# A four-layer diffusion trunk step: two projections as one f32 product each, one mask less, norm weights as columns, a shorter inverse root

## The chip, the cores and the metric

One core of one Trainium2 chip runs one program that holds the whole step. The metric is device time in microseconds (us) from the first to the last instruction of the core, with what lies around it; lower is better. Times of the kernel before are the median of three runs and one profiled execution.

## The reference

128 prompt tokens (s = 0) and 128 sample tokens (s = 1) of width 1024 go through four layers. Layer 0 mixes tokens with a gated DeltaNet, layer 1 with neighbourhood attention, layer 2 with latent attention (low-rank keys and values), layer 3 with RWKV-7. Each layer then applies a SwiGLU feed-forward of inner width 2816. Before each sub-layer stands a root-mean-square norm, modulated by a shift and scale from an adaptive matrix (`ada_w`). All inputs are float32. The parts that the change touches:

```python
def rmsnorm(x, g):
    y = x * lax.rsqrt(jnp.mean(x * x, -1, keepdims=True) + NORM_EPS)
    return y * g
...
# every sub-layer: x += gate * f(rmsnorm(x) * (1 + scale) + shift)
def chunk_gated_delta(q, k, v, g, beta, s0):
    ...
    a_mat = jnp.where(strict, jnp.einsum('...id,...jd->...ij', kb, k) * decay, 0.0)
    sol = lax.linalg.triangular_solve(a_mat + jnp.eye(DN_CHUNK), rhs, left_side=True, lower=True, unit_diagonal=True)
...
def deltanet_mixer(h, s0, w_in, w_gate, ..., out_norm, w_out):
    q, k, v, z = jnp.split(h @ w_in, 4, -1)
    ...
    o = rmsnorm(o, out_norm) * jax.nn.silu(z.reshape(b, t, DN_HEADS, DN_DIM))
    return o.reshape(b, t, -1) @ w_out, s
...
def na_project(h, w_qkv, q_norm, k_norm):
    qkv = (h @ w_qkv).reshape(b, t, 3, NA_HEADS, NA_DIM).transpose(2, 0, 3, 1, 4)
    return rmsnorm(qkv[0], q_norm), rmsnorm(qkv[1], k_norm), qkv[2]
...
def mla_project(h, w_a, q_a_norm, kv_a_norm, w_q_b, q_norm):
    cq, ckv, kpe = jnp.split(h @ w_a, [MLA_Q_LORA, MLA_Q_LORA + MLA_KV_LORA], -1)
    q = (rmsnorm(cq, q_a_norm) @ w_q_b).reshape(b, t, MLA_HEADS, MLA_NOPE + MLA_ROPE)
    return rmsnorm(q, q_norm).transpose(0, 2, 1, 3), rmsnorm(ckv, kv_a_norm), kpe
...
def rwkv_step(s, inp):
    r, w, k, v, a, bb = inp
    sa = jnp.einsum('...ij,...j->...i', s, a)
    s = s * w[..., None, :] + sa[..., :, None] * bb[..., None, :] + v[..., :, None] * k[..., None, :]
    return s, jnp.einsum('...ij,...j->...i', s, r)
...
    return (y * g) @ w_out, s        # end of rwkv_mixer
```

## The kernel before, in words

**One recorded program.** The Python code does not issue instructions directly. A `Recorder` (L84) writes every engine operation to a `Tape` (L64); `Plan` (L1753) then sorts all operations of all engines with a table of engine costs and free buffers, over several rounds (`Plan.best`, L2071), and `emit` issues the order that it judges best, all from L2133. So every instruction of the profile has one line, and a change of one operation sorts the whole program anew: work with no dependence on its neighbours, above all the adaptive matrix, can move by hundreds of instructions.

**Products.** A large projection is kept near float32 accuracy in three fp32r products. `weight` (L304) loads a 128x1024 piece over SyncE's queue, and `split` (L285) makes two halves of it: ScalarE copies the raw weight to fp32r (hi), VectorE subtracts that from the raw weight (lo). `linear` (L320) then issues, for each of two token groups and each k tile of 128, hi·hi, hi·lo and lo·hi, each a matmul with 512 columns. The activations are split in the same way (`norm_T` L456, `to_T` L414, `split_T` L422). `linear_k` (L377) has a mode `whole` already: one f32 product on the raw weight, used for RWKV's r, k and v. `out_half` (L481) is the projection out of a mixer, half of its input width at a time, whose result `residual` (L486) adds to x.

**Filler.** `ada_group` (L243) computes the adaptive matrix: for each k tile four concurrent matmuls of 32 stationary and 512 moving columns, with 1 MB of `ada_w` per load. Nothing in the mixer waits for it, so the planner puts it where TensorE would be idle.

**Norms and inverse roots.** `normed` (L432) reads the sums of squares, calls `rsqrt` (L149) for a 128x1 column, scales x and transposes it. `rsqrt` is 11 VectorE instructions: a scaled sum, a shift and a multiply-add on the bits, and two rounds of four.

**DeltaNet** (`deltanet_`, L704). `linear` at L866 computes z (chunks 6 and 7 of `dn_w_in`) and its gate. `inverses` (L650) inverts the triangular matrices of the delta rule: ScalarE gathers 32x32 diagonal blocks, VectorE transposes them (`inverse_base`, L586) and does a substitution of 31 steps with two instructions each (`substitute`, L602), then TensorE continues with 32x32 and 64x128 products. TensorE can do other work only if the planner has some left.

**Attention** (`neighbourhood_` L1044, `latent_` L1139). `rms_heads` (L976) multiplies each head by its inverse root and then by the norm's weight, both on VectorE; `transposed` (L984) transposes heads on TensorE and copies them out of PSUM on ScalarE.

**RWKV-7** (`rwkv_`, L1255). It works in two halves of the heads (g = 0, 1). `rw_products` (L1614) forms key products AT, which VectorE multiplies by a strict triangular mask out of PSUM; `inverses` is used on these too, once per half; `rw_core` (L1629) solves and applies the state, `rw_out` (L1713) normalises, and `out_half` projects with `rw_w_out` (L1494, L1502).

## Time and profile before

| what | value |
|---|---|
| timed runs | median 1655.51 us (1654.04 to 1658.28, three runs) |
| profiled execution | 1659.55 us, span of the core 1657.8 us |
| TensorE (PE) busy | 1577.0 us, 95% of the span, 11320 records |
| weight loads (PEld) busy | 1295.8 us, 78% |
| VectorE (DVE) busy | 1097.0 us, 66% |
| ScalarE (ACT) busy | 811.7 us, 49% |
| mean granted TensorE clock | 0.978 |

The trace gives, for each instruction, start, length, and what released it if its engine had been idle; "v" stands for any tile of the program, since tile names carry numbers. A matmul of f32 operands leaves two records in PE and two weight loads in PEld, one of fp32r operands one each. The records of both say "f32".

### The profile page before, as it was taken

Reading aid. Unit: us, or ns where it says so; the run is one execution under the profiler, and the core shown is the slowest. Engines: PE = TensorE matmul, PEld = TensorE weight load, DVE = VectorE, ACT = ScalarE, POOL = GpSimd, SP = SyncE. Lnnn points to the kernel's source line nnn. Section 1 sums busy time; section 2 is a strip of 40 time slices with the busy share of each in tenths; the row PEclk is TensorE's granted clock in tenths of the full one; section 3 lists DMA queues with packets and bytes.
Section 4 is the critical chain, followed back from the end, with each engine's and each line's share of the span. In section 5 each row is a group of like instructions: output and inputs, shape, how many; then the busy total and the mean of one; then the engine's idle time right before and its main releaser. Section 6 shows DMA issues by size and latency. Waiting matters only on the chain. (4 is left out here: it accounts for less than half of the span.)

```text
span 1657.8 us, 28812 instructions
## 1 busy us (share of the span) xinstructions
PE 1577.0 (95%) x11320; PEld 1295.8 (78%) x11320; DVE 1097.0 (66%) x2294; ACT 811.7 (49%) x1405; POOL 71.7 (4%) x137
## 2 busy tenths in 40 slices
PE   7999699999999999999999999999999699989998
PEld 3986377998778779987776799885757388879986
DVE  4887786444597874455997744547883898765444
ACT  4795365434466763344666644433633442454343
POOL 2001010000002000000110000000000000000000
PEclk9999799999999999999999999999999879999999
DMA  9768787558667675566767845666071421345554
GB/s 353 276 242 290 290 274 280 190 153 288 225 246 189 232 260 152 167 203 201 262 196 265 292 153 166 215 207 238 16 292 41 158 87 62 100 151 154 166 191 140
DMA packets 132792, 334.03 MB, mean 201 GB/s; under 512 B 18465, under 2 KB 32594, under 8 KB 121392
## 3 DMA queue, kind: packets, MB, share of 16 engines
q1 hardware_dynamic: 125936, 311.33, 54.9%
q0 software_dynamic: 6720, 20.86, 4.4%
q8 instruction: 89, 1.46, 0.4%
q14 instruction: 47, 0.39, 0.1%
HBM read 328.25 MB, written 3.90 MB: 200 GB/s over the span
## 5 line engine op out<-in xcount | busy, mean ns | idle before, releaser
L2133 PE MATMUL v<-v,v 128*128 128x256 f32 (+12 forms) x11288 | 1571.5, 331 | 74.9 <-DVE v L2133 34.2
L2133 PEld LDWEIGHTS v<-v,v 128*128 128x128 f32 (+8 forms) x11288 | 1290.1, 173 | 354.0 <-issue 123.9
L2133 DVE TENSOR_TENSOR v<-v,v 128x512 f32<-128x512 f32 (+16 forms) x1244 | 856.1, 714 | 480.9 <-ACT v L2133 328.3
L2133 ACT ACTIVATE v<-v 128x1024 fp32r<-128x1024 f32 (+14 forms) x972 | 674.6, 732 | 782.1 <-PE v L2133 316.1
L2133 ACT ACTIVATE v<-v,v 128x128 f32<-128x128 f32 (+2 forms) x172 | 65.6, 434 | 21.7 <-DVE v L2133 14.0
L2133 ACT ACTIVATE v<-v,v,v 128x128 f32<-128x128 f32 (+2 forms) x136 | 55.8, 495 | 35.1 <-DVE v L2133 34.2
L2133 DVE SCALAR_TENSOR_TENSOR v<-v,v,v 128x128 f32<-128x128 f32 (+4 forms) x152 | 59.1, 446 | 6.0 <-ACT v L2133 3.8
L2133 DVE TENSOR_REDUCE v<-v 128x4 f32<-128x512 f32 (+4 forms) x76 | 47.0, 626 | 8.3 <-PE v L2133 4.8
L2133 POOL DMA_DIRECT2D v<-v x22 | 11.8, 539 | 765.8 <-DVE v L2133 405.0
L2133 DVE TENSOR_SCALAR v<-v 128x1 int32<-128x1 int32 (+11 forms) x202 | 35.0, 177 | 6.2 <-ACT v L2133 3.7
L2133 DVE SCALAR_TENSOR_TENSOR v<-v,v 128x4 f32<-128x4 f32 (+6 forms) x172 | 34.0, 211 | 5.2 <-ACT v L2133 3.3
L2133 POOL MEMSET v<- 128x512 f32 (+6 forms) x49 | 21.4, 446 | 365.5 <-DVE v L2133 143.1
L2133 DVE SCALAR_TENSOR_TENSOR v<-v 128x1 f32<-128x1 f32 (+4 forms) x171 | 26.4, 162 | 1.9
L2133 DVE STREAM_TRANSPOSE v<-v 128x1024 f32<-128x1024 f32 x12 | 23.5, 2009 | 5.4 <-ACT v L2133 5.2
L2133 DVE TENSOR_SCALAR v<-v,v,v 128x128 f32<-128x128 f32 x64 | 24.7, 405 | 3.3 <-PE v L2133 2.9
L2133 ACT ACT_TABLE_LOAD x18 | 23.1, 1283 | 4.0 <-DVE v L2133 3.0
L2133 DVE TENSOR_SCALAR v<-v,v 128x512 f32<-128x512 f32 (+2 forms) x68 | 24.3, 389 | 0.2
L2133 DVE TENSOR_TENSOR v<-v 128x1 f32<-128x1 f32 (+4 forms) x74 | 11.8, 160 | 11.2 <-ACT v L2133 10.2
L2133 DVE COPY v<-v 128x32 f32<-128x32 f32 (+7 forms) x23 | 4.9, 211 | 13.3 <-PE v L2133 13.1
L2133 ACT ACTIVATION_READ_ACCUMULATOR v<-v,v 128x1 f32 x64 | 13.3, 207 | 0.0
L2133 DVE RECIPROCAL v<-v 128x2 f32<-128x2 f32 (+2 forms) x25 | 4.5, 181 | 7.7 <-ACT v L2133 7.6
L2133 POOL DMA_DIRECT2D v<-rw_w x10 | 6.0, 601 | 59.4 <-DVE v L2133 58.5
(38 smaller groups left out, 62.6 us busy)
## 6 DMA issues: line engine op xcount, KB each, us to landing
v<-ada_w SPq DMA_DIRECT2D x88, 1024.0 KB
v<-ffn_w_in SPq DMA_DIRECT2D x160, 512.0 KB
v<-ffn_w_out SPq DMA_DIRECT2D x88, 512.0 KB
v<-dn_w_in SPq DMA_DIRECT2D x32, 512.0 KB
v<-na_w_qkv SPq DMA_DIRECT2D x24, 512.0 KB
v<-rw_w_rkv SPq DMA_DIRECT2D x24, 512.0 KB
v<-v POOLq DMA_DIRECT2D x20, 512.0 KB, 4.9
v<-ada_w SPq DMA_DIRECT2D x16, 512.0 KB
```

Source lines behind the costliest of these rows:

```text
L2133: ins = getattr(getattr(nc, engine), method)(*[real(a) for a in args], **{k: real(a) for k, a in kw.items()}).ins
```

## The change

It has four parts. First, `WHOLE = ("dn_z", "rw_out")`: z of DeltaNet and RWKV's projection out become one f32 product on raw weights; `norm_T` keeps the unsplit activations for it, and RWKV's output is no longer split. (The diff also offers the same for the projections of latent attention, which is not switched on.) Second, `rw_products` copies AT out of PSUM on ScalarE without the mask. Third, the weights of the q and k norms become columns that scale ScalarE's copy in `transposed`; the multiplies of VectorE stay only where the new cache needs the weighted keys (two in neighbourhood attention) and for the 32 rotated columns of the sample tokens in latent attention (four of 128x4x32). Seven small loads on GpSimd's queue fill the columns. Fourth, `rsqrt` merges the shift into the multiply (minus a half), and for a single column needs three instructions a round: 8 instead of 11, and 10 instead of 11 elsewhere.

```diff
         with self.scope():
             m, y, t, v = [self.g(shp) for _ in range(4)]
-            h, yi = t.bitcast(I32), y.bitcast(I32)
-            nc.vector.tensor_scalar(m, x, scale / k ** 2, eps / k ** 2, op0=OP.mult, op1=OP.add)
-            nc.vector.tensor_scalar(h, m.bitcast(I32), 1, None, op0=OP.logical_shift_right)
-            nc.vector.tensor_scalar(yi, h, -1.0, float(0x5f3759df), op0=OP.mult, op1=OP.add)
+            single = shp[1] == 1
+            carry = k ** 6 if single else k ** 2
+            nc.vector.tensor_scalar(m, x, scale / carry, eps / carry, op0=OP.mult, op1=OP.add)
+            nc.vector.tensor_scalar(y.bitcast(I32), m.bitcast(I32), -0.5, float(0x5f3759df), op0=OP.mult, op1=OP.add)
             for last in (False, True):
+                if single:
+                    f = k if last else 1.0
+                    nc.vector.scalar_tensor_tensor(t, y, y, m, op0=OP.mult, op1=OP.mult)
+                    nc.vector.scalar_tensor_tensor(v, t, -10.0 / 3 / f, t, op0=OP.add, op1=OP.mult)
+                    nc.vector.scalar_tensor_tensor(out if last else y, v, 5.0 / f ** 2, y, op0=OP.add, op1=OP.mult)
+                    continue
                 if last:
...
-    def linear(self, W, chunks, xs, evac, lags=None):
+    def linear(self, W, chunks, xs, evac, lags=None, whole=False):
...
-                held[t] = self.weight([W[k0 * 128:(k0 + n) * 128, a:b] for a, b in chunks[ci]], n, width)
-            hi, lo = held[t]
+                held[t] = (self.raw_weight if whole else self.weight)([W[k0 * 128:(k0 + n) * 128, a:b] for a, b in chunks[ci]], n, width)
             if k0 == 0:
                 acc[s] = self.ps()[:, :width]
             for kk in range(n):
                 k = k0 + kk
+                if whole:
+                    nc.tensor.matmul(acc[s], xs[s](k), held[t][:, kk, :], start=(k == 0), stop=(k == nk - 1))
+                    continue
+                hi, lo = held[t]
                 xh, xl = xs[s](k)
...
+        if lo is None:
+            self.nc.scalar.activation(hi, v, AF.Copy, **({} if gain is None else {"scale": gain}))
+            return
...
+                if keep:
+                    h = hs[g][:, :, s]
+                else:
+                    own = self.g([128, 4, 128])
+                    h = own
...
-    def out_half(self, W, oT, g, gates):
-
-        xs = [lambda k, s=s: (oT[0][g][:, k, s, :], oT[1][g][:, k, s, :]) for s in range(2)]
-        self.linear(W[g * 512:g * 512 + 512], [[(0, 512)], [(512, 1024)]], xs, self.residual(gates, g == 1), OUT)
+    def out_half(self, W, oT, g, gates, whole=False):
+
+        xs = [lambda k, s=s: oT[0][g][:, k, s, :] if whole else (oT[0][g][:, k, s, :], oT[1][g][:, k, s, :]) for s in range(2)]
+        self.linear(W[g * 512:g * 512 + 512], [[(0, 512)], [(512, 1024)]], xs, self.residual(gates, g == 1), OUT, whole)
...
+WHOLE = ("dn_z", "rw_out")
...
-        self.linear(W, [[(c * 512, c * 512 + 512)] for c in (6, 7)], xs, gating, IN)
-        self.free(ht)
+        if "dn_z" in WHOLE:
+            self.free(ht)
+            self.linear(W, [[(c * 512, c * 512 + 512)] for c in (6, 7)], [lambda k, s=s: hs[k // 4][:, k % 4, s] for s in range(2)], gating, IN, True)
+            self.free(hs)
+        else:
+            self.linear(W, [[(c * 512, c * 512 + 512)] for c in (6, 7)], xs, gating, IN)
+            self.free(ht)
...
-        nc.vector.tensor_tensor(x, x, gain[:, None, :].to_broadcast([128, nh, hd]), op=OP.mult)
+        if gain is not None:
+            nc.vector.tensor_tensor(x, x, gain[:, None, :].to_broadcast([128, nh, hd]), op=OP.mult)
...
-        nc.scalar.activation(dst, p[:w, :n * 128].rearrange("p (a b) -> p a b", b=128), AF.Copy)
+        nc.scalar.activation(dst, p[:w, :n * 128].rearrange("p (a b) -> p a b", b=128), AF.Copy, **({} if gain is None else {"scale": gain}))
...
-        gq, gk = self.g([128, 64]), self.g([128, 64])
-        self.bcast_row(gq, I["na_q_norm"][j])
+
+        for i, nm in enumerate("qk"):
+            for e in range(2):
+                nc.gpsimd.dma_start(gc[64 * e:64 * e + 64, i:i + 1], I[f"na_{nm}_norm"][j].rearrange("(p o) -> p o", o=1))
+        nc.vector.tensor_scalar(gc[:, 0:1], gc[:, 0:1], 0.125, None, op0=OP.mult)
...
-                self.rms_heads(heads(t), 8, 64, gq if ci < 2 else gk)
+                own = ci >= 2 and s == 0
+                self.rms_heads(heads(t), 8, 64, gk if own else None)
                 g = slice(ci % 2 * 4, ci % 2 * 4 + 4)
                 dst = qT[s][:, g] if ci < 2 else k0T[:, g] if s == 0 else k1T[ci % 2][:, :, 0]
-                self.transposed([t[:, i * 128:(i + 1) * 128] for i in range(4)], 4, dst)
...
+        nc.gpsimd.memset(gc, 1.0)
+        nc.gpsimd.dma_start(gc[0:96, 0:1], I["mla_q_norm"][j].rearrange("(p o) -> p o", o=1))
+        nc.gpsimd.dma_start(gc[0:64, 2:3], I["mla_k_norm"][j, 0:64].rearrange("(p o) -> p o", o=1))
+        nc.vector.tensor_scalar(gc[0:96, 0:1], gc[0:96, 0:1], gc[0:96, 2:3], 96 ** -0.5, op0=OP.mult, op1=OP.mult)
+        nc.vector.tensor_copy(gc[0:64, 1:2], gc[0:64, 0:1])
...
-                self.rms_heads(q, 4, 96, gq)
+                self.rms_heads(q, 4, 96)
                 if s == 1:
+                    nc.vector.tensor_tensor(q[:, :, 64:96], q[:, :, 64:96], gq[:, None, :].to_broadcast([128, 4, 32]), op=OP.mult)
                     self.rope(q[:, :, 64:96], 4)
-                self.transposed([q[:, i] for i in range(4)], 4, qT[s][ci // 2][:96, ci % 2 * 4:ci % 2 * 4 + 4])
+                self.transposed([q[:, i] for i in range(4)], 4, qT[s][ci // 2][:96, ci % 2 * 4:ci % 2 * 4 + 4], gc[:96, s:s + 1])
...
-                nc.vector.tensor_tensor(f["AT"][s][e], p[e].rearrange("p (i t) -> p i t", i=4),
-                                        self.K(f"mstr{d}")[:, None, :].to_broadcast([128, 4, 128]), op=OP.mult)
+                nc.scalar.activation(f["AT"][s][e], p[e].rearrange("p (i t) -> p i t", i=4), AF.Copy)
...
-        self.to_T(yy, 4, oT[0][g][:, :, s, :], oT[1][g][:, :, s, :])
+        self.to_T(yy, 4, oT[0][g][:, :, s, :], None if "rw_out" in WHOLE else oT[1][g][:, :, s, :])
```

**The new order.** Since the planner sorts anew, three stretches of the order show where work has moved. In the rows, an operation stands as output<-inputs with its shape, `x4` for four alike.

TensorE (PE), layer 0: the end of the work ahead of the inversion's 32x32 products, before the change. `v_1749` and `v_1716` are sums of z (weights `v_1670`, `v_1677` with their lo halves `v_1679`, `v_1687`; activations `v_370`, `v_431`), `v_1751` and `v_1966` the adaptive matrix, `v_1910` a product with the old state, `v_2054` the first 32x32 product.

```order
L2133 MATMUL v_1751<-v_1756,v_63 32x512 x4
L2133 MATMUL v_1749<-v_1670,v_431 128x512
L2133 MATMUL v_1749<-v_1677,v_370 128x512
L2133 MATMUL v_1749<-v_1687,v_370 128x512
L2133 MATMUL v_1749<-v_1677,v_431 128x512
...
L2133 MATMUL v_1751<-v_1870,v_63 32x512 x4
L2133 MATMUL v_1910<-v_1648,v_1308 128x128
L2133 MATMUL v_1966<-v_1896,v_63 32x512 x4
L2133 MATMUL v_1966<-v_1920,v_63 32x512 x4
L2133 MATMUL v_1966<-v_1935,v_63 32x512 x4
L2133 MATMUL v_2003<-v_75,v_1961 128x128 x4
...
L2133 MATMUL v_2054<-v_2012,v_1600 32x32 x2
```

And with the change, the same place: `v_1760` and `v_1713` are the sums of z, `v_1833` the adaptive matrix, `v_1869` a product with the old state, `v_1917` the first 32x32 product.

```order
L2187 MATMUL v_1760<-v_1531,v_273 128x512 x2
L2187 MATMUL v_1760<-v_1548,v_273 128x512 x2
L2187 MATMUL v_1760<-v_1563,v_371 128x512
...
L2187 MATMUL v_1713<-v_1576,v_371 128x512 x2
L2187 MATMUL v_1833<-v_1673,v_63 32x512 x4
L2187 MATMUL v_1833<-v_1741,v_63 32x512 x4
L2187 MATMUL v_1833<-v_1755,v_63 32x512 x4
L2187 MATMUL v_1869<-v_1378,v_1326 128x128
...
L2187 MATMUL v_1833<-v_1865,v_63 32x512 x4
L2187 MATMUL v_1917<-v_1875,v_1559 32x32 x16
```

Between the last key product of the DeltaNet and the first 32x32 product there stood 48 fp32r products of z, 56 matmuls of the adaptive matrix, 24 products with the old state and 12 transposes; there now stand 30 f32 products of z, 24 of the adaptive matrix, 29 with the old state and 8 transposes. Over the whole program, 28 matmuls of the adaptive matrix leave the DeltaNet; RWKV, neighbourhood attention and layer 1's feed-forward get 12 more each.

ScalarE (ACT), layer 3: the copies that gather the 32x32 blocks (`32x128`) for the second inversion, before the change. Their sources `v_13299` to `v_13376` are VectorE's eight masked tiles AT; `v_13190` and `v_13198` belong to the decays, `v_13327` to a copy of the queries.

```order
L2133 ACTIVATE v_13190<-v_13190,v_12061,v_12057 128x256 x3
L2133 ACTIVATE v_13311<-v_13299 32x128 x4
L2133 ACTIVATE v_13327<-v_13304 128x512
L2133 ACTIVATE v_13311<-v_13307 32x128 x4
L2133 ACTIVATE v_13311<-v_13320 32x128 x4
...
L2133 ACTIVATE v_13311<-v_13376 32x128 x4
L2133 ACTIVATE v_13198<-v_13198,v_12061,v_12057 128x256 x2
L2133 ACTIVATE v_13441<-v_13413 128x256
```

And with the change: `v_13052`, `v_13061`, `v_13069`, `v_13076`, `v_13122` and others like them are now AT itself, copied from PSUM by ScalarE, and `v_13087` is the gathered tile.

```order
L2187 ACTIVATE v_13069<-v_13047 128x512
L2187 ACTIVATE v_13076<-v_13050 128x512
L2187 ACTIVATE v_13087<-v_13052 32x128
L2187 ACTIVATE v_13087<-v_13061 32x128
...
L2187 ACTIVATE v_12992<-v_12793 64x512
L2187 ACTIVATE v_13087<-v_13052 32x128
...
L2187 ACTIVATE v_13122<-v_13063 128x512
L2187 ACTIVATE v_13130<-v_13065 128x512
L2187 ACTIVATE v_13087<-v_13122 32x128
...
L2187 ACTIVATE v_13148<-v_13080 128x512
```

The eight copies of 128x512 have joined the 32 gathering copies on ScalarE, in one queue; VectorE's eight mask multiplies, which stood between these products and its transposes, are gone.

## Rows read from the trace of the kernel before

**Rows 1.** The page: busy time, then PE in 40 slices of the span.
```profile
PE 1577.0 (95%) x11320; PEld 1295.8 (78%) x11320; DVE 1097.0 (66%) x2294; ACT 811.7 (49%) x1405; POOL 71.7 (4%) x137
PE   7999699999999999999999999999999699989998
```

**Rows 2.** Waits of PE over the span: us, times, longest.
```profile
PE v L2133 <- DVE v L2133: 34.2, 21, 10.2
PE v L2133 <- DMA v<-ada_w: 15.1, 14, 3.4
```

**Rows 3.** Groups by form: xcount | busy us, mean ns | idle before.
```profile
L2133 DVE TENSOR_TENSOR v<-v,v 128x1024 fp32r<-128x1024 f32 x373 | 452.6, 1223 | 345.5 <-ACT v L2133 294.7 <-PE v L2133 43.9 <-issue 2.3
L2133 ACT ACTIVATE v<-v 128x1024 fp32r<-128x1024 f32 x373 | 391.2, 1058 | 429.1 <-DMA v<-ffn_w_in 203.0 <-DMA v<-ffn_w_out 95.3 <-PE v L2133 58.8
L2133 DVE TENSOR_TENSOR v<-v,v 128x512 f32<-128x512 f32 x329 | 216.0, 685 | 75.4 <-PE v L2133 60.7 <-ACT v L2133 9.7 <-DMA v<-na_rel_bias 2.5
L2133 ACT ACTIVATE v<-v 128x512 f32<-128x512 f32 x248 | 143.4, 613 | 235.9 <-PE v L2133 181.9 <-DVE v L2133 49.8 <-DMA v<-x_prompt 2.4
L2133 DVE TENSOR_TENSOR v<-v,v 128x384 f32<-128x384 f32 x16 | 8.7, 549 | 0.0
L2133 DVE TENSOR_SCALAR v<-v 128x1 int32<-128x1 int32 x40 | 6.0, 150 | 0.7
```

**Rows 4.** Windows: us, busy (x) of PE, PEld, DVE, ACT, POOL; PEclk, DMA, GB/s.
```profile
1060.00:1110.00 50.00, 49.91 (x215) 39.81 (x214) 24.21 (x21) 19.56 (x19) 1.89 (x3) 1.00 0.58 188
1130.00:1155.00 25.00, 25.00 (x60) 11.13 (x59) 16.13 (x47) 5.42 (x14) 0.88 (x1) 1.00 0.53 194
```

**Rows 5.** Timeline of PEld in an f32 stretch: start, us.
```profile
1150.12 0.19 PEld L2133 LDWEIGHTS v<-v,v 128*128 128x128 f32 x1 [0.24 <-issue]
1150.55 0.19 PEld L2133 LDWEIGHTS v<-v,v 128*128 128x128 f32 x1 [0.24 <-issue]
```

**Rows 6.** Windows around the DeltaNet inversion.
```profile
160.00:180.00 20.00, 10.28 (x80) 5.86 (x82) 18.39 (x50) 1.87 (x4) 1.06 (x2) 0.77 0.81 311
180.00:200.00 20.00, 13.70 (x324) 8.08 (x320) 15.83 (x51) 8.12 (x14) 0.00 (x0) 0.84 0.82 304
```

**Rows 7.** Timeline of PE in the DeltaNet inversion, 164 to 190.
```profile
163.75 4.77 PE L2133 MATMUL v<-v,v 128*128 128x128 f32 x36
178.24 4.73 PE L2133 MATMUL v<-v,v 128*32 128x512 f32 x28 [9.72 <-DVE v L2133]
185.45 1.07 PE L2133 MATMUL v<-v,v 128*32 128x512 f32 x8 [2.48 <-DMA v<-ada_w]
```

**Rows 8.** Timeline of PE, RWKV second inversion, 1290 to 1328.
```profile
1304.84 2.53 PE L2133 MATMUL v<-v,v 64*64 64x64 f32 x24 [2.78 <-ACT v L2133]
1325.99 1.11 PE L2133 MATMUL v<-v,v 64*64 64x64 f32 x8 [10.17 <-DVE v L2133]
```

**Rows 9.** Timeline of ACT before that inversion.
```profile
1292.56 10.83 ACT L2133 ACTIVATE v<-v 32x128 f32<-32x128 f32 x33
```

**Rows 10.** Timeline of DVE in that inversion.
```profile
1303.43 3.86 DVE L2133 STREAM_TRANSPOSE v<-v 128x1024 f32<-128x1024 f32 x2 [3.73 <-ACT v L2133]
1308.72 17.51 DVE L2133 TENSOR_TENSOR v<-v,v 128x31 f32<-128x31 f32 x44
```

**Rows 11.** Windows after that inversion, 20 us each.
```profile
1320.00:1340.00 20.00, 13.80 (x86) 13.03 (x87) 19.19 (x45) 1.21 (x3) 0.53 (x1) 0.50 0.18 59
1340.00:1360.00 20.00, 19.00 (x378) 17.62 (x377) 19.52 (x41) 15.07 (x23) 0.53 (x1) 0.79 0.21 62
1360.00:1380.00 20.00, 19.62 (x159) 15.94 (x159) 18.55 (x41) 3.80 (x7) 2.69 (x5) 1.00 0.25 67
1380.00:1400.00 20.00, 20.00 (x216) 18.26 (x216) 17.52 (x29) 5.62 (x8) 0.54 (x1) 1.00 0.24 70
```

**Rows 12.** Timeline of PE at the end of RWKV.
```profile
1456.65 1.06 PE L2133 MATMUL v<-v,v 128*128 128x128 f32 x8 [3.71 <-DVE v L2133]
1458.74 1.65 PE L2133 MATMUL v<-v,v 128*128 128x512 f32 x3 [1.03 <-ACT v L2133]
```

More of the change, by code (lines that the diff above doesn't have):

```diff
@@ L454, in normed, with norm_T @@
                 yield g, p, gs[:, g, :], self.ada_col(l, 3 * which, s, g)
-    def norm_T(self, l, which):
+    def norm_T(self, l, which, keep=0):
         nc = self.nc
-        ht = self.h_tiles()
+        ht = self.h_tiles() if keep < 2 else None
+        hs = [self.g([128, 4, 2, 128]) for _ in range(2)] if keep else None
         for s in range(2):
             for g, p, gs, sh in self.normed(l, which, s):
-                h = self.g([128, 4, 128])
+                if keep:
[3 more added lines that the diff above has]
+                    h = own
+                if keep == 2:
+                    for i in range(4):
+                        q = p[:, i * 128:(i + 1) * 128]
+                        if i < NV:
+                            nc.vector.tensor_scalar(h[:, i, :], q, gs[:, i:i + 1], sh[:, i:i + 1], op0=OP.mult, op1=OP.add)
+                        else:
+                            nc.scalar.activation(h[:, i], q, AF.Identity, bias=sh[:, i:i + 1], scale=gs[:, i:i + 1])
+                    continue
                 hi = ht[0][g][:, :, s, :]
@@ L472, in norm_T @@
                 nc.vector.tensor_tensor(ht[1][g][:, :, s, :], h, hi.bitcast(F32), op=OP.subtract)
-                self.free(h)
-        return ht
+                if not keep:
+                    self.free(own)
+        return ht if not keep else (ht, hs) if keep == 1 else hs
     def sumsq(self, s, c):
@@ L705, in deltanet_ @@
         nc, I = self.nc, self.I
-        ht = self.norm_T(l, 0)
+        ht = self.norm_T(l, 0, 1 if "dn_z" in WHOLE else 0)
+        if "dn_z" in WHOLE:
+            ht, hs = ht
         xs = self.h_of(ht)
@@ L974, in head_rsqrt, with rms_heads @@
         return r
-    def rms_heads(self, x, nh, hd, gain):
+    def rms_heads(self, x, nh, hd, gain=None):
         nc = self.nc
@@ L1062, in evac @@
             if ci < 4:
-                self.rms_heads(heads(t), 8, 64, gq if ci < 2 else gk)
+                own = ci >= 2 and s == 0
+                self.rms_heads(heads(t), 8, 64, gk if own else None)
                 g = slice(ci % 2 * 4, ci % 2 * 4 + 4)
                 dst = qT[s][:, g] if ci < 2 else k0T[:, g] if s == 0 else k1T[ci % 2][:, :, 0]
-                self.transposed([t[:, i * 128:(i + 1) * 128] for i in range(4)], 4, dst)
+                self.transposed([t[:, i * 128:(i + 1) * 128] for i in range(4)], 4, dst, None if own else gc[:, ci // 2:ci // 2 + 1])
             if ci == 3 and s == 0:
@@ L1157, in latent_ @@
         nc.gpsimd.dma_start(ck[2][:, 256:288], I["cache_mla_kpe"][0, j])
-        cqT = [self.g([128, 3, 2, 128], F32R) for _ in range(2)]
-        ckT = [self.g([128, 2, 3, 128], F32R) for _ in range(2)]
-        self.to_T(ck[2], 2, ckT[0][:, :, 2], ckT[1][:, :, 2])
+        cqT = [self.g([128, 3, 2, 128], F32R) for _ in range(2)] if not wq else [self.g([128, 3, 2, 128])]
+        ckT = [self.g([128, 2, 3, 128], F32R) for _ in range(2)] if not wkv else [self.g([128, 2, 3, 128])]
+        self.to_T(ck[2], 2, ckT[0][:, :, 2], None if wkv else ckT[1][:, :, 2])
         kp, p1 = [self.g([128, 1, 32]) for _ in range(3)], [self.g([128, 1]) for _ in range(3)]
@@ L1211, in latent_ @@
         self.linear(I["mla_w_kv_b"][j], [[(c * 512, c * 512 + 512)] for c in range(4)],
-                    [lambda kk, s=s: (ckT[0][:, kk, s], ckT[1][:, kk, s]) for s in groups], evac, (1, 1, 1))
+                    [lambda kk, s=s: ckT[0][:, kk, s] if wkv else (ckT[0][:, kk, s], ckT[1][:, kk, s]) for s in groups], evac, (1, 1, 1), wkv)
         self.free(ckT)
@@ L1413, in core @@
             if d == 1:
-                for o in oT:
-                    o.append(self.g([128, 4, 2, 128], F32R))
+                if "rw_out" in WHOLE:
+                    oT[0].append(self.g([128, 4, 2, 128]))
+                else:
+                    for o in oT:
+                        o.append(self.g([128, 4, 2, 128], F32R))
             for s in range(2):
@@ L1493, in rwkv_ @@
         gates = [self.gate(l, 0, s) for s in range(2)]
-        self.out_half(I["rw_w_out"][j], oT, 0, gates)
+        self.out_half(I["rw_w_out"][j], oT, 0, gates, "rw_out" in WHOLE)
         if FP == 2:
@@ L1501, in rwkv_ @@
         self.free(v, y0)
-        self.out_half(I["rw_w_out"][j], oT, 1, gates)
+        self.out_half(I["rw_w_out"][j], oT, 1, gates, "rw_out" in WHOLE)
     def rw_decays(self, g, d, hid, w2):
```

30 lines of the change are left out of this document (18 added, 12 removed).

## The prediction

> **What bounds the kernel now.** I read the page first: TensorE (PE) is busy 95% of the span and VectorE (DVE) 66%, and the slices show PE full almost everywhere except in three places [rows 1]. So a change pays either by making PE's work cheaper or by closing PE's holes; work taken off DVE or ACT elsewhere is hidden. The waits say what opens the holes: DVE 34.2 us and loads of the adaptive matrix 15.1 us [rows 2]. The timelines say where. The largest are the two places where triangular matrices are inverted on DVE while PE runs out of filler: layer 0, 160 to 200 us, and the second inversion of RWKV, 1300 to 1328 us. In the first, PE is busy 10.28 and 13.70 of 20 us [rows 6], 16.0 us idle, and the longest wait is 9.72 us for DVE [rows 7]. In the second, PE waits 2.78 us for ACT and 10.17 us for DVE [rows 8]. DVE there runs 17.51 us of substitution without a pause, and started it late, since it had waited 3.73 us for ACT before its transposes [rows 10]; ACT was gathering blocks, 33 copies in 10.83 us [rows 9]. A third stretch, after that inversion, reads differently: in the four windows from 1320 DVE is busy 19.19, 19.52, 18.55 and 17.52 of 20 us [rows 11], so DVE and PE share the bound.
>
> **What each part costs.** The sum is made against the profiled execution, 1659.55 us; it lies 4.0 us above the median of the runs, so I subtract the result from 1655.5.
>
> *One f32 product in place of three fp32r.* 192 fp32r matmuls go and 64 f32 ones come. An fp32r matmul of 512 columns costs 49.91/215 = 0.232 us in a stretch that holds nearly nothing else [rows 4]. An f32 matmul is two records; in a stretch of these, one starts every 0.43 us (1150.12, 1150.55) [rows 5], so 0.86 us for the matmul. Three of the old kind are 0.696 us, so PE pays 0.164 us more each, 64 times: **+10.5 us**, half for z, half for the projection out. This is the one term against the change that is certain as work.
>
> A row to set beside this price: in the fp32r stretch the weight loads are busy 39.81 of 50 us, in the f32 stretch 11.13 of 25 [rows 4], while PE is full in both. The Trainium skill ("Perfetto Trace Analysis", Identifying the Most-Contended Engine) holds that matmul busy time says little about how near TensorE is to its limit, since matmuls are pipelined, and that weight-load busy time is the better measure. By that the change, with fewer loads, would make PE's work cheaper. The starts 0.43 us apart speak against it, since f32 instructions would not stand so far apart if loads set the pace, so I keep +10.5 and give the other reading a chance below.
>
> *Splits that go.* Sixteen weight splits leave, each 1.223 us on DVE and 1.058 on ACT [rows 3]: 19.6 and 16.9 us. Four splits of RWKV's output leave DVE, at the 0.685 us of its shape [rows 3], 2.7 us. DVE also loses 16 masks (16 x 0.685 = 11.0), six attention multiplies of the same shape (4.1) and eight of 128x384 (8 x 0.549 = 4.4). Twenty single-column inverse roots lose three instructions each and 37 others one, at 0.15 us [rows 3]: 14.6 us. DVE loses some 56 us in all; ACT loses 16.9 and gains 16 x 0.613 = 9.8 [rows 3]. Most of this lies under a full PE and is worth nothing; the places below are where it isn't.
>
> *The hole in layer 0.* The length of the chain there (ACT's gathering, DVE's transposes and substitution) does not change, as its instructions don't. What changes is the filler that PE has while it runs. Before: 48 x 0.232 (z) + 56 x 0.169 (adaptive matrix, 28 in 4.73 us, [rows 7]) + 24 x 0.265 (old state, 36 records in 4.77 us at two a matmul, [rows 7]) + 12 transposes at about the same 0.25 = 30.0 us. After: 30 x 0.86 + 24 x 0.169 + 29 x 0.265 + 8 x 0.25 = 39.5 us. The planner has put nearly all the dearer z product where PE had nothing, and sent adaptive work to other layers. So the idle falls by 9.5 of its 16.0 us. **-9.5.** Bounds: -16 if the late loads of `ada_w` (2.48 us, [rows 7]) vanish too; 0 if they come later than the filler needs them, as then the 32x32 products wait as before and the moved matmuls cost their time elsewhere.
>
> *The second inversion of RWKV.* DVE loses its eight masks (5.5 us), but ACT gets eight copies of 0.613, 4.9 us, in the queue that ended last: DVE waited for ACT, not for its own masks [rows 9, 10]. So the chain starts later: between +1 us (other ACT work moved away, the first copies run under the products) and +4.9. I take +3. Against it, the order shows DVE putting 2 us less of other work into the substitution, and PE having 20 more matmuls of the adaptive matrix (20 x 0.169 = 3.4 us) and some solves of the first half, about 7 us more filler in all. PE's idle there would fall by about 6, and the chain's delay of 1 net is within it: **-5**, with bounds -12 and +4.
>
> *After it.* DVE's load there falls by the eight splits of `rw_w_out` and four of the output, 8 x 1.223 + 2.7 = 12.5 us; PE pays 5.2 more in the same place (already in the +10.5). At the end of RWKV, PE waits 3.71 and 1.03 us for the norm chain [rows 12], which becomes three instructions of 0.15 us, with their gaps about 0.6 us, shorter and has fewer splits in its queue. Taken: **-2.5**; bounds 0 and -12.5.
>
> *Inverse roots elsewhere.* Each sub-layer begins with a norm whose chain of 11 is seen by PE only if its filler ends: of 16, I take three or four exposed, at 0.6 us: **-2**. Attention's multiplies stand between a head's inverse root and its transposes; of the 4.4 us that latent attention loses I take a third as seen by PE: **-1.5**. Both terms are judgement, with bounds 0 and -9 together (all 16 chains and the 4.4 us, less what overlaps). The seven small loads on GpSimd's queue are needed only after a projection of tens of microseconds, so nothing; if they were late, they would hold ACT's scaled copies by one load.
>
> Sum: +10.5 - 9.5 - 5 - 2.5 - 2 - 1.5 = -10.0 us, so 1655.5 - 10 = 1645.5; I say **1646**. The new order of everything adds scatter of some 4 us that I cannot price.
>
> **The rivals.**
> *ACT ends both of RWKV's inversions (slower).* The eight copies sit ahead of 32 gathering copies in one queue, so DVE's transposes start a full 4.9 us later, in both inversions: +9.8. The filler found for the second is adaptive matrix, whose loads are late already [rows 2]. Then -5 becomes +9.8, and the -2.5 after it goes, since DVE starts its crowded stretch later: 1655.5 + 10.5 - 9.5 + 9.8 - 3.5 = 1663. It decides from about 3 us per inversion. For it: DVE's 3.73 us wait was for ACT [rows 10]. Against it: 5.5 us of DVE leave the same path.
> *DVE is what bounds the second half of RWKV (more gain).* With 75 of 80 us busy after 1320 [rows 11], removing 12.5 us of DVE work there takes out most of it instead of 2.5: 1646 - 10 = 1636. The granted clock is 0.50 in the first of these windows, half rate after the hole, so a shorter hole returns some of it also. Against it: PE is full too from 1340 (19.00, 19.62, 20.00 of 20).
> *Nothing comes of it.* The filler put into layer 0's hole is missed where it came from, and only the roots and the projection out balance: gain of 2 to 4 us, 1653.
> *Weight loads pace PE.* If so, 192 - 128 = 64 loads fewer at 39.81/214 = 0.186 us [rows 4] are -11.9 in place of +10.5: 1646 - 22 = 1624. It is what the rule cited above from the Trainium skill ("Perfetto Trace Analysis", Identifying the Most-Contended Engine) would lead one to expect.
>
> **How the numbers follow.** A difference of 0.3%, 5 us, is about what a measurement of this kernel can tell from none. Chances: forecast 0.42 (1639 to 1653), more gain 0.16, nothing 0.18, ACT 0.18 (1659 to 1668), weight loads 0.06. Faster than 1650.5: four fifths of the forecast, 0.34, plus 0.16 and 0.06, is 0.56. Slower than 1660.5: most of ACT's case, 0.15, and a little of scatter, 0.02: 0.17. Within: 0.27. The range of 8 in 10 takes the forecast, "nothing", three quarters of "more gain" and half of ACT's case: 1630 to 1663.
>
> **What would show it.** PE's busy time should rise by about 9 to 11 us while its idle time, span less busy, falls from 80.8 us [rows 1] to about 60. In layer 0, the long wait for DVE (9.72 us) should shrink to a few us with f32 records in the place of fp32r. In RWKV's second inversion, ACT should show eight 128x512 copies among the 32x128 ones, and DVE's transposes a wait for ACT; if that wait or the gap before the 64x64 products is longer than the old 10.17 us, ACT's case holds. DVE below 95% busy after that inversion while PE is full speaks against "more gain". The prediction is wrong in its main term if PE's busy time does not rise, and in its second if the holes' idle time stays at 16 and 17 us.

## The result

The changed kernel is slower: 1665.96 us median of 20 runs against 1655.82 us, ratio 1.0053 (95% interval 1.0036 to 1.0071). The forecast was 1646 us, a gain. The profiled execution, 1657.65 us with a span of 1655.9, is the third shortest of the 20, which reach from 1653.99 to 1678.36 us, at a mean granted clock of 0.986 to 0.982 in the five up to 1663.32 us and of 0.979 to 0.973 in the others. This spread is itself a finding and is taken up below.

The page and the waits of the changed kernel, as [rows 1, 2] of before:

```profile
PE 1582.3 (96%) x11256; PEld 1285.6 (78%) x11256; DVE 1059.4 (64%) x2152; ACT 802.9 (48%) x1405; POOL 73.5 (4%) x143
...
PE v L2187 <- DVE v L2187: 29.8, 22, 11.0
PE v L2187 <- DMA v<-ada_w: 13.8, 14, 2.8
```

PE's busy time rose by 5.3 us, half of what was forecast, and span less busy fell by 7.2 us (80.8 to 73.6), a third of what was forecast. Busy time depends on the clock, though: the trace before has a mean clock of 0.978, this one 0.986. In two more traces of the changed kernel, at 0.984 (e1) and 0.979 (e5), PE is busy 1585.1 and 1591.1 us, 8.1 and 14.1 more than before. VectorE lost 37.6 us, some 19 less than its terms added up to.

The windows at the two inversions, as [rows 6, 11]. Layer 0 comes first, then RWKV:

```profile
160.00:180.00 20.00, 18.77 (x219) 11.19 (x219) 19.26 (x58) 6.36 (x11) 1.64 (x3) 1.00 0.49 182
180.00:200.00 20.00, 18.57 (x371) 15.82 (x364) 10.24 (x19) 14.64 (x24) 0.00 (x0) 0.83 0.70 264
...
1280.00:1300.00 20.00, 9.61 (x112) 6.15 (x109) 15.10 (x33) 4.98 (x18) 0.53 (x1) 0.83 0.75 266
1300.00:1320.00 20.00, 13.52 (x74) 7.56 (x76) 14.61 (x40) 0.60 (x1) 0.54 (x1) 0.67 0.75 289
1320.00:1340.00 20.00, 19.47 (x348) 14.88 (x347) 14.18 (x22) 9.73 (x16) 0.54 (x1) 0.91 0.40 123
1340.00:1360.00 20.00, 20.00 (x208) 15.69 (x207) 15.86 (x38) 5.30 (x9) 2.69 (x5) 1.00 0.42 130
```

Layer 0's hole is nearly closed: PE is idle 2.7 of 40 us where it was 16.0. RWKV's is as large as before. The timelines there, as [rows 8, 10], PE and then VectorE:

```profile
1300.61 4.07 PE L2187 MATMUL v<-v,v 128*32 128x512 f32 x24 [10.96 <-DVE v L2187]
1307.42 1.07 PE L2187 MATMUL v<-v,v 128*32 128x512 f32 x8 [2.75 <-DMA v<-ada_w]
1311.61 26.77 PE L2187 MATMUL v<-v,v 128*128 128x64 f32 x376 [3.12 <-DVE v L2187]
```
```profile
1282.96 3.84 DVE L2187 STREAM_TRANSPOSE v<-v 128x1024 f32<-128x1024 f32 x2 [7.53 <-ACT v L2187]
```

10.96 + 2.75 + 3.12 = 16.8 us of idle (before, the waits from 1302 to 1328 us made 16.7), and VectorE waited 7.53 us for ScalarE before its transposes, where it had been 3.73.

Length of each part in us, worked out from the traces (from the first matmul of a part's norm to that of the next; the first part begins with the span, the last ends with it; "z alone" is experiment e15):

| stretch | before | changed | changed, third trace (e5) | z alone |
|---|---|---|---|---|
| DeltaNet | 256.9 | 243.8 | 242.8 | 240.6 |
| its feed-forward | 198.6 | 199.0 | 199.8 | 200.2 |
| layers 1 and 2 up to latent attention's end | 469.2 | 469.6 | 467.3 | 468.9 |
| layer 2's feed-forward | 197.2 | 196.9 | 196.0 | 197.4 |
| RWKV | 334.7 | 337.4 | 347.0 | 332.8 |
| its feed-forward | 201.1 | 209.2 | 206.3 | 204.3 |

So the DeltaNet became 13 us shorter, and RWKV and its feed-forward 11 us longer, in a trace that lies 8 us below the median; no trace of this kernel is of an execution at its median. Nor are the 13 us all gain. The DeltaNet now holds 248 records of the adaptive matrix instead of 304. Eight of them take 1.07 us [rows 7], so these 56 are some 7.5 us of work that went elsewhere: layers 1 and 2 got 48 records, RWKV 24 and the feed-forward of layer 0 got 8, that of layer 2 lost 24.

### The profile page after: what moved, and what is told of

The parts are those of the page before. It is cut to its first block, busy times and chain, and to the rows that moved or that the text cites. A ratio compares the mean times of both kernels' runs of the same rounds, so it can differ in the third digit from the quotient of the medians.

```text
span 1655.9 us, 28539 instructions
## 1 busy us (share of the span) xinstructions
PE 1582.3 (96%) x11256; PEld 1285.6 (78%) x11256; DVE 1059.4 (64%) x2152; ACT 802.9 (48%) x1405; POOL 73.5 (4%) x143
## 4 chain that ended last, share of the span: by engine, by line
PE 71%; DMA 8%; DVE 5%; ACT 3%; issue 2%; POOL 0%; SPq 0%; ACTq 0%; DVEq 0%; POOLq 0%
PE v L2187 71%; DVE v L2187 5%; ACT v L2187 3%; DMA v<-ffn_w_out 3%; DMA v<-ada_w 3%; DMA v<-na_rel_bias 1%; DMA v<-ffn_w_in 1%; DMA v<-mla_w_q_b 0%; DMA v<-na_w_qkv 0%; DMA v<-rw_w_rkv 0%; ACT L2187 0%; DMA v<-rw_ln_b 0%; POOL v L2187 0%; SPq L2187 0%; ACTq L2212 0%
## 5 line engine op out<-in xcount | busy, mean ns | idle before, releaser
L2187 PE MATMUL v<-v,v 128*128 128x256 f32 (+14 forms) x11224 | 1575.2, 331 | 66.7 <-DVE v L2187 29.1
L2187 DVE TENSOR_TENSOR v<-v,v 128x1024 fp32r<-128x1024 f32 (+16 forms) x1157 | 812.6, 727 | 500.7 <-ACT v L2187 347.0
L2187 ACT ACTIVATE v<-v 128x1024 fp32r<-128x1024 f32 (+12 forms) x958 | 659.0, 727 | 768.5 <-PE v L2187 295.5
L2187 ACT ACTIVATE v<-v,v 128x128 f32<-128x128 f32 (+4 forms) x186 | 74.5, 458 | 33.3 <-DVE v L2187 27.4
L2187 DVE SCALAR_TENSOR_TENSOR v<-v,v 128x1 f32<-128x1 f32 (+5 forms) x212 | 42.6, 213 | 4.2 <-ACT v L2187 1.1
L2187 POOL MEMSET v<- 128x512 f32 (+7 forms) x50 | 20.5, 423 | 428.6 <-PE v L2187 262.8
L2187 DVE TENSOR_SCALAR v<-v 128x1 f32<-128x1 f32 (+11 forms) x146 | 25.9, 181 | 8.8 <-ACT v L2187 6.9
L2187 DVE SCALAR_TENSOR_TENSOR v<-v 128x4 f32<-128x4 f32 (+4 forms) x151 | 22.7, 159 | 1.9
L2187 DVE TENSOR_TENSOR v<-v 128x4 f32<-128x4 f32 (+5 forms) x54 | 8.7, 161 | 10.2 <-ACT v L2187 9.8
L2187 ACT ACTIVATION_READ_ACCUMULATOR v<-v,v 128x1 f32 x64 | 13.7, 214 | 0.0
```

The lines of the kernel that those rows point to most:

```text
L2187: ins = getattr(getattr(nc, engine), method)(*[real(a) for a in args], **{k: real(a) for k, a in kw.items()}).ins
```

## The experiments

**Other executions (e1, e5).** The changed kernel again.

> The changed kernel once more, for its times and for the trace of another execution. The profiled execution (1657.65 us, mean granted clock 0.986) was faster than the median of the 20 runs (1665.96, most at 0.973 to 0.979). Theory 'clock': a typical execution shows about 0.977 and is 8 us longer, with the extra time in stretches where the granted clock is at its lower level that were at full level in the first trace (near the inversions). Theory 'loads': a typical execution has the same clock pattern and more idle time of PE behind loads.

> The changed kernel a third time, for a trace of a typical execution: both traces so far are of executions near 1657 us at a granted clock of 0.985, while 25 of 30 runs are above 1660 at 0.973 to 0.982. Theory 'clock': at 1664 us or more the trace shows a stretch of some 15 to 40 us more at half clock, and it lies after RWKV's second inversion, where PE is full (the trace of the version with only z whole had one from 1335.7 to 1390.4, and 1678 us). Theory 'loads': the extra time is spread over the span as idle time of PE behind loads.

e1: 1668.58 us median of 10, ratio 1.0073 (1.0047 to 1.0098); its trace is of the shortest of these (1656.98). e5: 1661.05 us, clock 0.979, still 5 us below the median of the 20. Its windows:

```profile
1300.00:1320.00 20.00, 15.20 (x81) 8.13 (x73) 13.71 (x37) 0.60 (x1) 0.31 (x1) 0.59 0.88 318
1320.00:1340.00 20.00, 20.00 (x226) 15.47 (x228) 7.20 (x10) 8.56 (x14) 0.54 (x1) 0.50 0.21 64
```

The same instructions, in the same order, with the same wait of 10.97 us before them: in the window from 1320, PE is full and gets 226 records done at a granted clock of 0.50 (its 1.2 GHz level), against 348 at 0.91 in the first trace. The half clock lasts from 1304.1 to 1341.6 us here, from 1310.1 to 1323.7 there, behind a stretch of 10.2 us in both. RWKV takes 347.0 instead of 337.4 us. Idle time behind loads does not differ (12.6 and 13.8 us for `ada_w`). Theory "loads" falls; "clock" holds for the spread between executions of one kernel.

It does not hold for the difference between the two kernels. The trace of the kernel before has a half clock of the same length in the same place, from 1310.8 to 1348.4 us, and RWKV takes 334.7 us there; but PE was busy only 13.80 of 20 us in it [rows 11], where it is full in e5. And at a mean clock of 0.979 four of the 20 runs of the changed kernel take 1663.42 to 1668.56 us, and nine runs of the kernel before, timed beside e1, 1650.28 to 1659.62. So the work that a half clock falls on matters beside its length.

**Leaving parts of the change out, sorted anew (e2, e3, e4, e16).**

```diff
-WHOLE = ("dn_z", "rw_out")
+WHOLE = ()                     # e2;  e4 and e16: ("dn_z",)
...
-                nc.scalar.activation(f["AT"][s][e], p[e].rearrange("p (i t) -> p i t", i=4), AF.Copy)
+                nc.vector.tensor_tensor(f["AT"][s][e], p[e].rearrange("p (i t) -> p i t", i=4),
+                                        self.K(f"mstr{d}")[:, None, :].to_broadcast([128, 4, 128]), op=OP.mult)   # e3, e16
```

> The changed kernel with both products split again, in three fp32r matmuls (the other three parts stay). Theory 'price': the f32 products cost PE 10.5 us and little of it is covered, so the ratio to before falls from 1.0053 to about 0.999 or below (1654 us or less). Theory 'ACT copies': the loss lies in RWKV's inversions, so it stays at 1.003 or more. Theory 'order': any new order of the program moves the time by some 5 us either way; then it can be anywhere within 1.000 +- 0.006 and says little by itself.

> The changed kernel with the mask back: 16 multiplies on VectorE in place of ScalarE's copies of AT. Theory 'ACT copies': VectorE waited 7.53 us for ScalarE before its transposes, against 3.73 in the kernel before, so with the mask back the wait falls to about 3.7 and the time by 4 to 9 us (ratio 0.998 to 1.003). Theory 'price': no gain, ratio 1.004 to 1.007.

> The changed kernel with z of DeltaNet as one f32 product but RWKV's projection out split again. Theory 'price', with the cover that the order shows: z fills layer 0's hole (13 us earlier at the start of the first feed-forward in the trace of the changed kernel), the projection out pays 5 us uncovered, so the ratio falls by 0.003 to 0.005, to about 1.001. Theory 'ACT copies': the same as the changed kernel, 1.004 to 1.007.

> The changed kernel without two parts: RWKV's projection out split again and the mask on VectorE again; z whole, norm columns and short roots stay. Theory 'parts': RWKV is then that of the kernel before (335 us) and the time 1638 to 1648, ratio 0.990 to 0.996. Theory 'order': a stretch of half clock of 40 us or more behind RWKV's second inversion is there or not by the order, so it is 1650 to 1665 with a wide spread.

e2: 1674.89, ratio 1.0115 (1.0086 to 1.0144). e3: 1661.47, 1.0037 (1.0018 to 1.0056); VectorE's wait before its transposes is 3.72 us again, as "ACT copies" expected, and the median is 4 to 7 us below those of the changed kernel, though the intervals overlap. e4: 1659.41, 1.0048 (1.0018 to 1.0078), spread 1654.57 to 1678.09. e16: 1659.38, 1.0035 (1.0016 to 1.0055). Theory "price" does not come true in e2: with the products split again the time is 6 to 9 us longer, with layer 0's hole open (PE busy only 7.13 us in the window from 160) and a half clock of 61.4 us in RWKV. Nor does "parts" in e16, which expected 0.990 to 0.996. The trace of e4 fell on 1678.09 us and shows the worst case of the same effect, PE full for 40 us at half clock:

```profile
1340.00:1360.00 20.00, 20.00 (x100) 16.96 (x96) 10.49 (x18) 3.30 (x4) 0.00 (x0) 0.50 0.06 23
1360.00:1380.00 20.00, 20.00 (x114) 16.77 (x114) 8.64 (x21) 3.35 (x5) 3.22 (x6) 0.50 0.31 85
```

**The order alone (e7, e8).** The same instructions in the next orders on the planner's list.

```diff
-    _, order, turns, _ = min(Plan(tape).best(ROUNDS, WAITS), key=lambda x: x[0])
+    _, order, turns, _ = sorted(Plan(tape).best(ROUNDS, WAITS), key=lambda x: x[0])[1]   # e8: [2]
```

> The kernel before with the planner's second-best order in place of its best: the same instructions. Theory 'order': the order that the kernel before has is a lucky one of many, and another costs 5 to 15 us: ratio 1.003 to 1.01. Against it: the order matters less than 0.3%, ratio 0.997 to 1.003.

> The changed kernel with the planner's third-best order in place of its best: the same instructions as the changed kernel. Theory 'order': the time moves by 5 us or more, to either side (below 1660 or above 1672). Against it: it stays within 1666 +- 4, and the loss belongs to the instructions.

e7: 1661.29, 1.0044 (1.0024 to 1.0065). e8: 1659.69, 1.0031 (1.0002 to 1.0060), some 6 us below the changed kernel by the medians, with intervals that overlap. So another order of the very instructions of the kernel before costs 7 us (4 to 11 by the interval), nearly what the whole change costs. Any experiment that sorts anew carries this scatter (e2 to e4, e6, e9 to e12, e15, e16 and e18), and none of them can price a part to 5 us.

**PE kept busy (e6, e9 to e12).** 18 (e10: 9) f32 matmuls of no use, tied to the place between the transposes and the 32x32 products of RWKV's second inversion; their sum is overwritten.

```diff
         nc.vector.copy_predicated(A, self.bmask, A2)
+        self.px = None
+        if warm:
+            self.px = self.ps()
+            for i in range(warm):
+                nc.tensor.matmul(self.px, A[:, :4].rearrange("p a b -> p (a b)"), A[:, 16:].rearrange("p a b -> p (a b)"),
+                                 start=True, stop=True)
```

> The changed kernel with 18 f32 matmuls of 128x512 more, on data that nobody needs, on PE between the transposes of RWKV's second inversion and the 32x32 products (18 x 0.43 x 2 = 15.5 us of PE's time). Theory 'clock': PE does not fall idle there, so the half clock after it (1293 to 1324, and the longer stretch in typical runs) is gone; the time falls to 1652 to 1660 although PE works 15 us more. Theory 'price' or 'loads': the 15.5 us are paid, wholly or in part: 1668 to 1682.

> The changed kernel with 9 idle matmuls instead of 18 (7.7 us of PE's time). Theory 'clock': half of the hole stays, so some half clock remains and the time lies between: 1650 to 1660, with a wider spread than with 18. If it is at 1645 or below, 18 were more than needed.

> The kernel before with the same 18 idle matmuls in RWKV's second inversion. It has a half clock of 37.6 us there too (1310.8 to 1348.4). Theory 'clock alone': with that stretch gone from both kernels what is left is the worth of the instructions; if the change is worth the 10 us that were forecast, this kernel is at 1655 or above, ratio 0.998 to 1.004, against 0.9963 for the changed kernel with them. Theory 'no worth': it gains as much as the changed kernel did, to 1640 to 1650, ratio 0.99 to 0.997.

> The changed kernel with both products split again and 18 idle matmuls: with the clock of RWKV's second inversion out of the comparison, it prices the f32 products against e6 (1649). Theory 'cover': layer 0's hole opens again (19.09 us of waiting in the trace of e2) and costs more than the 10.5 us that the fp32r form saves: 1652 to 1662. Theory 'price': 1640 to 1646.

> The changed kernel with the mask on VectorE again and 18 idle matmuls. Theory 'ACT copies': with PE kept busy the later start of the substitution still costs some us, so this is 2 to 6 us faster than e6 (1643 to 1647). Theory 'clock alone': the wait for ScalarE mattered only through the clock, so it is the same as e6 within 3 us.

e6 (on the changed kernel): 1649.16, 0.9963 (0.9945 to 0.9981), 17 us less than the changed kernel although PE does 15.5 us more. Its windows:

```profile
1280.00:1300.00 20.00, 20.00 (x184) 12.66 (x187) 14.68 (x31) 6.96 (x24) 1.06 (x2) 1.00 0.95 358
1300.00:1320.00 20.00, 20.00 (x138) 10.07 (x138) 18.87 (x49) 1.82 (x3) 0.54 (x1) 1.00 0.89 336
1320.00:1340.00 20.00, 19.87 (x381) 16.20 (x380) 14.85 (x35) 10.92 (x18) 1.61 (x3) 1.00 0.32 105
1340.00:1360.00 20.00, 20.00 (x84) 13.76 (x85) 12.58 (x28) 2.42 (x4) 1.62 (x3) 0.66 0.16 43
```

No hole, full clock through it (a half clock of 13.7 us follows from 1342.5), RWKV of 335.3 us, and twelve runs within 6.4 us (1645.77 to 1652.14). e10 with 9: 1652.63, 0.9992 (0.9971 to 1.0013), with a wider spread (1643.03 to 1661.49), as expected. This looked like proof that the clock is the whole cause. e9 says no: on the kernel before, the same matmuls cost 20 us, 1673.72, 1.0118 (1.0088 to 1.0147), and the half clock did not go, it moved behind the hole to 1352.0 to 1389.5 us, where PE is full:

```profile
1340.00:1360.00 20.00, 17.58 (x286) 14.50 (x285) 17.46 (x31) 9.27 (x15) 1.59 (x3) 0.80 0.21 54
1360.00:1380.00 20.00, 20.00 (x161) 17.55 (x160) 10.70 (x23) 5.92 (x9) 1.61 (x3) 0.50 0.24 80
```

It began within a wait of PE for VectorE, of 2.42 us. Not all of the 20 us is these matmuls: e9 is sorted anew, and its DeltaNet, which holds none of them, takes 263.8 us for 256.9. e11 (products split): 1672.02, 1.0107 (1.0080 to 1.0133). e12 (mask on VectorE): 1666.78, 1.0071 (1.0047 to 1.0095), although its clock was 0.984 to 0.989; both lie above what either of their theories expected. Against the same version without them, the 18 matmuls are worth -17 us in the changed kernel, -3 with the products split (e11, e2), +5 with the mask back (e12, e3) and +20 in the kernel before; so theory "clock alone" falls as an account of the difference between kernels.

**One part in an unchanged order (e13, e14).** The program is sorted as before, and only at issue are the operations of one part replaced (e13: the mask multiplies by ScalarE's copies; e14: 11 instructions of a root by 8).

```diff
+        if i in tape.alt:                      # in emit
+            if tape.alt[i] is None:
+                continue
+            engine, method, args, kw = tape.alt[i]
...
+                nc.alt[len(nc.ops) - 1] = ("scalar", "activation", (f["AT"][s][e], p[e].rearrange("p (i t) -> p i t", i=4), AF.Copy), {})
```

> The kernel before in its own order, with one thing changed: the 16 mask multiplies of VectorE are issued as ScalarE's copies of AT at the same places of the order; nothing is sorted anew. Theory 'ACT copies': the substitution of RWKV's second inversion starts some 4 us later, PE's wait for VectorE grows from 10.17 to about 14 us, the time by 3 to 8 us (ratio 1.002 to 1.005). Theory 'order': the part by itself is worth nothing, 0.998 to 1.002, and the loss comes with the new order.

> The kernel before in its own order, with the 20 single-column inverse roots in 8 instructions instead of 11; nothing is sorted anew. Forecast as in the prediction: three or four exposed chains of 0.6 us, -2 us (ratio 0.998 to 1.000). Theory 'order': the same, since the order is kept; so if this gains and the changed kernel lost, the loss is not from the roots.

e13: 1658.44, 1.0038 (1.0016 to 1.0061): the mask part alone costs, 6 us by the ratio (3 to 10) and 3 us between the medians, which two long runs of twelve (1666.34 and 1673.66, clock 0.974 and 0.973) hardly move. VectorE and ScalarE ahead of the second inversion, as [rows 9, 10]:

```profile
1299.90 3.83 DVE L2138 STREAM_TRANSPOSE v<-v 128x1024 f32<-128x1024 f32 x2 [11.71 <-ACT v L2138]
```
```profile
1287.44 12.43 ACT L2138 ACTIVATE v<-v 128x512 f32<-128x512 f32 x34
```

VectorE now waits 11.71 us for ScalarE. From the start of RWKV (1121.9 us before, 1112.9 here) the transposes stand at 181.5 before and 187.0 us here, 5.5 us later, and RWKV takes 340.1 instead of 334.7 us. In e14, in the same order with the mask on VectorE, these are 181.5 and 334.3 us, so the 5.5 us are no scatter between executions. At the first inversion the delay is 0.8 us (72.8 to 73.6). PE's wait behind the transposes did not grow (9.02 for 10.17 us), as PE's work ahead of it is late as well; the delay is paid in length, not in the wait that was expected to show it. e14: 1652.15, 0.9992 (0.9969 to 1.0015): the roots are worth between -5 and +2 us, and the 60 instructions that go took 4.7 us off VectorE's busy time, where 9 had been counted.

**Parts that gain (e15, e17, e18).** The kernel before with z whole alone (e15); that order with short roots put in as in e14 (e17); both products whole and nothing else (e18).

> The kernel before with z of DeltaNet as one f32 product and none of the other parts, sorted anew. In every order so far the DeltaNet was 10 to 15 us shorter with z whole (242 to 247 us against 257 to 264). Theory 'parts': this part gains, RWKV stays as before (335 us), the time is 1640 to 1648, ratio 0.991 to 0.996. Theory 'order': RWKV's clock gives it back, 1655 to 1668.

> The version with z alone, in its own order, with the 20 single-column inverse roots in 8 instructions; nothing is sorted anew against it. If the parts add, the 1 to 3 us that the roots gained in the order of the kernel before come on top of z's 7 us: 1644 to 1648, ratio 0.993 to 0.997. Where the clock behind RWKV's second inversion decides, the spread stays 1644 to 1663 and the median within 2 us of z alone (1648).

> The kernel before with both f32 products (z and RWKV's projection out) and none of the other parts, sorted anew; against z alone (1648) it prices the projection out. Theory 'price': 32 f32 matmuls cost 5.2 us more and nothing covers them: 1651 to 1656. Theory 'splits': the 12.5 us that leave VectorE in RWKV's second half pay: 1638 to 1646. Theory 'order': the clock behind the inversion comes out another way: 1658 or more.

e15: 1648.13, 0.9977 (0.9952 to 1.0002); eight of twelve runs lie at 1644.33 to 1649.35 with a clock of 0.982 to 0.985, four at 1654.34 to 1662.54 with 0.974 to 0.977. e17: 1646.89, **0.9955 (0.9939 to 0.9971)**: with e6 the fastest version here, clear of both kernels. e18: 1663.33, 1.0046 (1.0028 to 1.0063), and its trace does not put the loss where the projection out stands: RWKV takes 331.7 us, no longer than before, but layer 1's feed-forward 210.2 (198.5 in z alone) and the DeltaNet 249.0, with 40 more matmuls of the adaptive matrix (320 records for 240). The loss thus lies where no instruction has changed, which points to the order; it was not tried in a fixed one. The projection out keeps its price of 5.2 us of PE's work, and whether anything covers it stays open.

## Why the prediction was wrong

**Right: the price.** In layer 0's z product a record starts every 0.43 us (139.84, 140.27, 140.70), so 0.86 us a matmul as forecast:

```profile
139.84 0.19 PEld L2187 LDWEIGHTS v<-v,v 128*128 128x128 f32 x1 [0.24 <-issue]
140.27 0.19 PEld L2187 LDWEIGHTS v<-v,v 128*128 128x128 f32 x1 [0.24 <-issue]
140.70 0.19 PEld L2187 LDWEIGHTS v<-v,v 128*128 128x128 f32 x1 [0.24 <-issue]
```

At a mean clock like that before (e5), PE's busy time is 14.1 us higher, where 10.5 were forecast, though more of the half clock falls on a full PE in e5. The reading by weight loads is out: their busy time is 0.19 us of each 0.43, and in all it fell by 10.2 us while the time rose by 10. By the Trainium skill ("Perfetto Trace Analysis", Identifying the Most-Contended Engine) loads are the better measure of how near TensorE is to its limit; for this trade of three short matmuls for one slow one, the trace says they are not a measure of time.

**Right in place, wrong in its sum: layer 0, "-9.5".** The hole went almost wholly (16.0 to 2.7 us), near the bound of -16. But the sum does not give that. Its 0.169 us is the time of a record (28 records in 4.73 us, [rows 7]), and an f32 matmul of the adaptive matrix leaves two, as the same sum reckons for the old state. At 0.338 us a matmul the filler goes from 39.4 to 43.6 us, 4.2 more and not 9.5. What closed the hole is seen in the traces: before, 79 of z's 96 records ran ahead of the inversion's transposes (at 153.6 us) and 17 behind them; now 15 of its 64 run ahead (at 140.2 us) and 49 behind. The inversion begins 13.4 us sooner, and z runs under it; the prediction's count began at the last key product and so took in z that had run ahead of the inversion. That -9.5 lies between the mended sum and the measured -13.3 is luck. Over the whole stretch idle time fell by 6.9 us only (27.4 to 20.5), as 4.3 us were added in the first 40 us of the program. The half clock in this place shrank as well, from 17.0 us in three stretches (170.8 to 201.5) to 6.8 (183.7 to 190.5), a gain that had no term.

**Wrong: the second inversion of RWKV, "-5".** The step that failed is "+3 for the later start, against about 7 us more filler", from which PE's idle time was to fall by about 6. It was 16.7 us and stayed 16.8.

The filler came too late. From the start of the transposes to the first 32x32 product there are 20 more matmuls of the adaptive matrix, as forecast: 80 records for 40. But only 48 of the 80 lie ahead of the hole's end at 1311.61 us. The other 32 run behind it, where PE has no gap left:

```profile
L2187 PE MATMUL v<-v,v 128*32 128x512 f32 x32 | 6.0, 833 | 0.0
```

The chain did not shorten. VectorE's own work in it did fall by some 2 us, as the order had shown (34.3 to 32.1 us busy). But from its first transposes to those behind the substitution it took 39.3 us instead of 34.5, since work of VectorE that needs a product of PE stands ahead of the latter and waits for it, 5.50 us in each of the three traces of this kernel:

```profile
1289.07 26.49 DVE L2187 TENSOR_TENSOR v<-v,v 128x31 f32<-128x31 f32 x69 [0.91 <-PE v L2187]
1321.07 1.29 DVE L2187 TENSOR_TENSOR v<-v,v 128x512 f32<-128x512 f32 x2 [5.50 <-PE v L2187]
1322.27 1.92 DVE L2187 STREAM_TRANSPOSE v<-v 128x1024 f32<-128x1024 f32 x1
```

And the later start: with the order held (e13) the transposes come 5.5 us later, more than the bound of 4.9. In the changed kernel VectorE waits 7.53 us for ScalarE there, yet the new order begins the whole inversion sooner, 173.7 us after the start of RWKV instead of 181.5. So the later start is shown as a cost for the order of the kernel before; in the new order what is shown is the filler that came behind the hole.

This is the place of the rival "ACT ends both inversions", given 0.18: in e13 it is right for the second, wrong for the first (0.8 us). That the measured time lies in its window (1659 to 1668) is partly luck. Putting the mask back does not help in every order: e3 is 4 to 7 us below the changed kernel, e12 is 18 us above e6.

**Wrong: "after it, -2.5" and the rival of more gain.** VectorE fell from 74.8 busy us of 80 [rows 11] to 57.6 in the windows from 1320, PE is full there, and RWKV did not get shorter: by the prediction's own sign VectorE is no bound there. At the end PE's wait for the norm chain did fall, 3.71 us to 1.61 at the longest, but in e14, where only the roots are shorter, it is 3.58. The last feed-forward became 5 to 8 us longer, with 4.6 us of waiting for ScalarE and VectorE from 1470 us on (0.9 before). There is no adaptive matrix there to cover it, but there was none before either; why it waits more was not tried.

**Wrong: the order as a footnote of "some 4 us".** It is as large as any other term: e7 moves the kernel before by 7 us with no instruction changed. The clock is part of the price of an order: the half clock behind the inversion lasted from 13.6 to 61.4 us in traces of these kernels, over full PE in the worst of them. The rows of before gave half a sign of it (0.50 in the window from 1320, [rows 11]), which the prediction used only as a gain, in a rival. What decides how long it lasts stays open.

What adds up, by the ratios: z -4 us (-8 to 0; e15, in an order of its own), roots -1 (-5 to +2; e14), mask +6 (+3 to +10; e13), together about +1; by the medians it is -7, -3 and +3, together -7. The measured change is +9 by the ratio and +10 by the medians. So 8 us or more belong to the projection out, the norm columns and the order that all parts get together; this was not split further, and the cause of the larger part stays open. The norm columns were not tried alone. Against them as a cause, layers 1 and 2 hold 296 records of the adaptive matrix in z alone and in the changed kernel, and take 468.9 us without the columns and 469.6 with them. For them, e16 has the columns and is 13 us slower than e17, which has not; but these two differ in 37 further roots and in the order as well.

## What to carry to other kernels

Where a planner sorts the whole program anew at each edit, price a part by putting it into the unchanged order first; only then let it sort, and compare several orders, since one order against another was worth nearly as much here as the edit. Count filler by where it stands against the start and the end of the wait, not by how much of it lies between two products, and keep records and matmuls apart when pricing it. Work moved off a busy engine onto an idle one is not free if the idle one has the last word at a wait: look who released it. And fill a hole of TensorE with work that has to be done anyway: in layer 0 both the idle time and the half clock became shorter.

## What was not expected of the hardware

One binary, one order, and executions 24 us apart (1653.99 to 1678.36), which go with the mean granted clock (0.986 to 0.973). In the first trace the clock fell within the wait of 10.96 us, came back to full after 10.2 us (1293.0 to 1303.2), fell again within the wait of 3.12 us, and stayed at half for 13.6 us; in another execution it stayed there for 37.5, with PE at work nearly all the while. Idle matmuls in that hole gained 17 us in one order and cost 20 in another, where a half clock of 37.5 us began within a wait of 2.42 us behind them. Why the stretch is short in one execution and long in the next stays open.
